# Input projection with one 512-column matmul for the high weights and seven banks drained by ScalarE

## The chip, the core and the metric

The kernel runs on one core of a Trainium2 chip. Its engines work side by side: PE (TensorE) multiplies, DVE (VectorE), ACT (ScalarE) and POOL (GpSimd) work element by element, SP (SyncE) issues the transfers. The metric is the device time of one execution in microseconds (us), as the median of the runs.

## The reference

The model has two layers on a sequence of 512 tokens with 2048 features, in float32. Only the first line of the first layer is touched by the change: a projection from 2048 to 8192 features, whose first half (`u`) is pooled over the sequence and whose second half gates it.

```
h = rmsnorm(x, norm_g)
proj = h @ w_in                       # (512, 2048) @ (2048, 8192)
u, gate = proj[..., :W_A], proj[..., W_A:]
pooled = causal_mean_pool(u, w) - u   # windows 2, 4, 8, 16 by group
y = einsum(pooled, w_group) * scale * silu(gate)
x = x + y @ w_out
# then the second layer: keys and values, latent attention, output projection
```

## The kernel before

**Numbers in two parts.** A float32 operand is split into a high part in PE's reduced float32 format (`hi`, written by ACT as a cast) and the rest (`lo`, written by DVE as a subtraction). A product is then three matmuls: high by high, high by low, low by high.

**Seven products instead of eight.** The projection multiplies blocks of 2x2 in the manner of Strassen and Winograd. The 64 output tiles (128 features by 512 tokens) are taken in pairs. Two of the 32 pairs are computed plainly in an opening stage, which also loads x and builds its seven combinations for each of the 8 blocks j of the inner dimension (`xh[j]`, `xl[j]`: 128 partitions, seven pieces of 256 tokens). The other 30 pairs follow in a loop (`n` = 0 to 29, pairs 18 to 31 and then 0 to 15). A pair has four quarters (`q`), each of two blocks j.

For each quarter `w_combos` loads 2 x 256 KB of weights into `raw` (three buffers), adds up four combinations (two in one instruction on DVE, line 301, then two on POOL, lines 303 and 304), casts all seven to `hi` on ACT (line 307) and subtracts to `lo` on DVE (line 308); `hi` and `lo` have two buffers each. `seven` then issues 42 matmuls of 256 columns (lines 324, 326, 328): seven products, two blocks, three matmuls each. The products gather in four banks of PSUM (`k0` to `k3`; two products to a bank, seven halves used), each with two buffers.

When the last quarter of a pair is done, `gather` adds the seven sums up: ACT copies one (line 334), DVE adds the others to it straight from PSUM (lines 335 to 338) into the tile `e` (two buffers), and SP stores two output tiles to DRAM (line 347). For the last loads, pairs 0 to 3 (`n` = 14 to 17), DVE also pools the outputs before they are stored (`pool_tile`, lines 240 to 256). The first eight rounds also square x on ACT and add the squares on DVE; in round 8 DVE works out the norm from them (lines 155 to 160 and 168).

**Order.** Each engine runs its own queue in order. The order of each queue is laid down when the program is built, by a scheduler that goes through a modelled timeline; waits are by semaphores between the engines. A tile's buffer is reused when all that used it has finished.

Of the kernel before, what the change touches and what calls it, by code (L numbers as in the profile page):

```python
# [51 lines left out]
def trunk_kernel(  # L52
# [50 lines left out]
    def dram():  # L103
        return dpool.tile([P, S], F32, tag="scr", name="scr", bufs=64)
# [154 lines left out]
    with ExitStack() as c1:  # L259
        xcp = c1.enter_context(tc.tile_pool(name="xcp", bufs=NJ))  # L260
        w7 = c1.enter_context(tc.tile_pool(name="w7", bufs=2, **tile_))
        ps7 = c1.enter_context(tc.tile_pool(name="ps7", bufs=2, space=bass.MemoryType.PSUM))
        xh, xl = [None] * NJ, [None] * NJ

        def x_load(j):

# [4 lines left out]

        def x_parts(j, c, hp):

            h = xcp.tile([P, 7, H], F32R, tag="xh", name="xh")
            lo = xcp.tile([P, 7, H], F32R, tag="xl", name="xl")
            xh[j], xl[j] = h, lo
            h12 = hp.tile([P, H], F32R, tag="h12", name="h12", bufs=NJ)
            l12 = hp.tile([P, H], F32R, tag="l12", name="l12", bufs=NJ)
            A.activation(c[:, 2:8:5, :], c[:, 2:8:5, :], AF.Copy, scale=cs[:, C_GA + 2 * j:C_GA + 2 * j + 1])
            A.activation(c[:, 0:2, :], c[:, 0:2, :], AF.Copy, scale=cs[:, C_GA + 2 * j + 1:C_GA + 2 * j + 2])  # L280
            A.copy(h[:, 0:3, :], c[:, 0:3, :])
            V.tensor_tensor(lo[:, 0:3, :], c[:, 0:3, :], f(h[:, 0:3, :]), ALU.subtract)
            split(c[:, 7, :], h12, l12)
            return h12, l12

        def x_sums(j, c):
            h, lo = xh[j], xl[j]
            V.tensor_tensor(c[:, 3:5, :], c[:, 1:3, :], c[:, 7:8, :].broadcast_to([P, 2, H]), ALU.subtract)
            V.scalar_tensor_tensor(c[:, 5, :], c[:, 4, :], -1.0, c[:, 1, :], ALU.mult, ALU.subtract)
            V.scalar_tensor_tensor(c[:, 6, :], c[:, 5, :], -1.0, c[:, 0, :], ALU.mult, ALU.subtract)  # L290
            A.copy(h[:, 3:7, :], c[:, 3:7, :])
            V.tensor_tensor(lo[:, 3:7, :], c[:, 3:7, :], f(h[:, 3:7, :]), ALU.subtract)

        def w_combos(pair, q):

            c = w7.tile([P, 2, 8, P], F32, tag="raw", name="raw", bufs=3)
            for m in range(2):
                nc.sync.dma_start(c[:, :, 2 - 2 * m:4 - 2 * m, :],
                                  awin[2 * pair + m][:, q * S:(q + 1) * S].rearrange(
                                      "p (j k n) -> p j k n", j=2, k=2))  # L300
            V.tensor_tensor(c[:, :, 4:6, :], c[:, :, 0:1, :].broadcast_to([P, 2, 2, P]),  # L301
                            c[:, :, 1:3, :], ALU.add)
            G.tensor_tensor(c[:, :, 6, :], c[:, :, 4, :], c[:, :, 2, :], ALU.add)  # L303
            G.tensor_tensor(c[:, :, 7, :], c[:, :, 6, :], c[:, :, 3, :], ALU.add)
            hi = w7.tile([P, 2, 7, P], F32R, tag="hi", name="hi")
            lo = w7.tile([P, 2, 7, P], F32R, tag="lo", name="lo")
            A.copy(hi, c[:, :, 1:8, :])  # L307
            V.tensor_tensor(lo, c[:, :, 1:8, :], f(hi), ALU.subtract)  # L308
            return hi, lo

        def banks():
            return [ps7.tile([P, 2, H], F32, tag=f"k{i}", name=f"k{i}") for i in range(4)]


        SEVEN = ((2, 0, 0, 0), (0, 6, 1, 0), (1, 2, 2, 0), (3, 4, 3, 0),
                 (5, 5, 0, 1), (6, 1, 1, 1), (4, 3, 2, 1))

        def seven(ks, w, j):
            hi, lo = w
            for wi, xi, b, h in SEVEN:  # L320
                dst = ks[b][:, h, :]
                first, last = j == 0 and h == 0, j == NJ - 1

                T.matmul(dst, hi[:, j % 2, wi, :], xh[j][:, xi, :], start=first, stop=False,  # L324
                         skip_group_check=True)
                T.matmul(dst, hi[:, j % 2, wi, :], xl[j][:, xi, :], start=False, stop=False,  # L326
                         skip_group_check=True)
                T.matmul(dst, lo[:, j % 2, wi, :], xh[j][:, xi, :], start=False, stop=last,  # L328
                         skip_group_check=True)

        def gather(ks, pair):

            e = epool.tile([P, 7, H], F32, tag="e", name="e")
            A.copy(e[:, 6, :], ks[2][:, 0, :])
            V.tensor_tensor(e[:, 0:2, :], e[:, 6:7, :].broadcast_to([P, 2, H]), ks[0], ALU.add)
            V.tensor_tensor(e[:, 2, :], e[:, 1, :], ks[2][:, 1, :], ALU.add)
            V.tensor_tensor(e[:, 3:6:2, :], e[:, 1:3, :], ks[3][:, 0:1, :].broadcast_to([P, 2, H]), ALU.add)
            V.tensor_tensor(e[:, 4:7:2, :], e[:, 2:4, :], ks[1], ALU.add)
            for i, v in enumerate((e[:, 0:7:6, :], e[:, 4:6, :])):
                o = 2 * pair + i  # L340
                raws[o] = dram()
                if i:
                    neg.add(o)
                if o < 8:
                    nc.sync.dma_start(raws[o], pool_tile(v, i == 1, WINS[0]))
                else:
                    nc.sync.dma_start(raws[o].rearrange("p (h t) -> p h t", h=2), v)


        accs = [ps7.tile([P, 2, H], F32, tag=f"k{i}", name=f"k{i}") for i in range(4)]  # L350
        with ExitStack() as c2:
            hp = c2.enter_context(tc.tile_pool(name="hp", bufs=2, **tile_))
            for j in range(NJ):
                c = x_load(j)
                raw = hp.tile([P, 4, 2, P], F32, tag="hraw", name="hraw")
                hi = w7.tile([P, 4, 2, P], F32R, tag="hi", name="hi")
                lo = w7.tile([P, 4, 2, P], F32R, tag="lo", name="lo")
                for o in range(4):
                    nc.sync.dma_start(raw[:, o, :, :], awin[32 + o][:, 2 * j * P:2 * (j + 1) * P].rearrange(
                        "p (k n) -> p k n", k=2))  # L360
                h12, l12 = x_parts(j, c, hp)
                for o in (0, 2):
                    split(raw[:, o:o + 2], hi[:, o:o + 2], lo[:, o:o + 2])
                x_sums(j, c)
                a, b = xh[j], xl[j]
                for o in range(4):
                    for dst, k, h, l in ((accs[o][:, 0, :], 0, a[:, 2, :], b[:, 2, :]),
                                         (accs[o][:, 1, :], 0, h12, l12),
                                         (accs[o], 1, a[:, 0:2, :], b[:, 0:2, :])):
                        first = j == 0 and h is not h12 and k == 0  # L370
                        T.matmul(dst, hi[:, o, k, :], h, start=first, stop=False, skip_group_check=True)
                        T.matmul(dst, hi[:, o, k, :], l, start=False, stop=False, skip_group_check=True)
                        T.matmul(dst, lo[:, o, k, :], h, start=False, stop=j == NJ - 1 and k == 1,
                                 skip_group_check=True)
        epool = c1.enter_context(tc.tile_pool(name="epool", bufs=2, **tile_))
        tp[0] = c1.enter_context(tc.tile_pool(name="tpool1", bufs=6, **tile_))
        for o in range(0, 4, 2):
            e = epool.tile([P, 7, H], F32, tag="e", name="e")
            for i in range(2):
                v = e[:, 2 * i:2 * i + 2, :]  # L380
                A.copy(v, accs[o + i])
                raws[32 + o + i] = dram()
                nc.sync.dma_start(raws[32 + o + i].rearrange("p (h t) -> p h t", h=2), v)

        sq = [tt_(), tt_()]

# [7 lines left out]
                V.tensor_tensor(sq[k % 2], sq[k % 2], x, ALU.add)  # L394

        for n, pair in enumerate((*range(18, 32), *range(16))):
            ks = banks()
            for q in range(NJ // 2):
                w = w_combos(pair, q)
                seven(ks, w, 2 * q)  # L400
                seven(ks, w, 2 * q + 1)
            if n < 8:
                square(2 * n)
                square(2 * n + 1)
            if n == 8:
                V.tensor_tensor(sq[0], sq[0], sq[1], ALU.add)
                p = ps7.tile([P, 2, H], F32, tag="k3", name="k3").rearrange("p h t -> p (h t)")
                ra[0] = norm_r(sq[0], D, p)
            gather(ks, pair)
# [526 lines left out]
```

## Time and profile before

| | |
|---|---|
| median of three runs | 1963.8 us (1961.78 to 1964.49) |
| the profiled execution | 1961.67 us, of which the span is 1959.9 us |
| granted PE clock | 0.999 |
| PE busy | 1933.3 us (99%), 11324 matmuls |
| DVE busy | 1280.2 us (65%) |
| ACT busy | 815.1 us (42%) |
| POOL busy | 262.9 us (13%) |

Rows of the page and of the groups read: line, engine, operation, output and inputs, shape, count, then busy us and mean ns. Rows of a timeline read: start in us from the span's start, duration in us, engine, line, operation, output and inputs; in square brackets stands how long the engine idled before and what ended that. Rows by stage read: the window, its length, then busy us and instruction counts of PE, PE's weight loads, DVE, ACT and POOL, then the granted clock and the transfers. The projection's loop runs from 55.5 to 667 us of the span.

### The profile page before, as it was taken

Reading aid. Unit: us, or ns where it says so; the run is one execution under the profiler, and the core shown is the slowest. Engines: PE = TensorE matmul, PEld = TensorE weight load, DVE = VectorE, ACT = ScalarE, POOL = GpSimd, SP = SyncE. Lnnn points to the kernel's source line nnn. Section 1 sums busy time; section 2 is a strip of 40 time slices with the busy share of each in tenths; the row PEclk is TensorE's granted clock in tenths of the full one; section 3 lists DMA queues with packets and bytes.
Section 4 is the critical chain, followed back from the end, with each engine's and each line's share of the span. In section 5 each row is a group of like instructions: output and inputs, shape, how many; then the busy total and the mean of one; then the engine's idle time right before and its main releaser. Section 6 shows DMA issues by size and latency. Waiting matters only on the chain.

```text
span 1959.9 us, 30545 instructions
## 1 busy us (share of the span) xinstructions
PE 1933.3 (99%) x11324; PEld 1707.0 (87%) x11324; DVE 1280.2 (65%) x2305; ACT 815.1 (42%) x1553; POOL 262.9 (13%) x404
## 2 busy tenths in 40 slices
PE   8999999999999999999999999999999999999999
PEld 7899999999999888888888888888888888878887
DVE  8766676797666587485694567573345888786432
ACT  7533333333333443333323454332245677774221
POOL 0432332334332100000000000000010111210000
PEclk9999999999999999999999999999999999999999
DMA  6644344435444464344344343233332111111632
GB/s 198 201 135 138 119 140 130 129 120 173 140 128 132 162 205 148 113 124 140 118 126 139 113 145 123 87 97 97 97 92 75 46 38 59 52 58 46 217 119 86
DMA packets 168134, 235.51 MB, mean 120 GB/s; under 512 B 14897, under 2 KB 95153, under 8 KB 167985
## 3 DMA queue, kind: packets, MB, share of 16 engines
q1 hardware_dynamic: 167696, 233.37, 37.9%
q8 instruction: 88, 1.44, 0.3%
q14 instruction: 62, 0.50, 0.1%
q10 hardware_dynamic: 288, 0.20, 0.0%
HBM read 208.35 MB, written 25.17 MB: 119 GB/s over the span
## 4 chain that ended last, share of the span: by engine, by line
PE 93%; DVE 3%; DMA 2%; issue 1%; ACT 1%; SPq 0%; DVEq 0%; ACTq 0%
PE mm L142 16%; PE mm L140 16%; PE mm L141 16%; PE k L328 9%; PE k L324 9%; PE k L326 9%; PE sc L728 3%; PE mm L604 1%; PE mm L602 1%; PE mm L603 1%; PE tr L687 1%; PE mm L622 1%; PE mm L624 1%; PE mm L623 1%; DVE lo L308 1%
## 5 line engine op out<-in xcount | busy, mean ns | idle before, releaser
L122 ACT CAST whi<-raw 128x512 fp32r<-128x512 f32 (+2 forms) x421 | 255.7, 611 | 518.9 <-PE mm L141 455.7
L324 PE MATMUL k<-xh,hi 128*128 128x256 f32 x1680 | 460.1, 283 | 0.1
L326 PE MATMUL k<-xl,hi 128*128 128x256 f32 x1680 | 460.0, 283 | 0.0
L123 DVE TENSOR_TENSOR wlo<-raw,whi 128x512 fp32r<-128x512 f32 (+2 forms) x421 | 281.9, 672 | 222.2 <-ACT whi L122 217.8
L328 PE MATMUL k<-xh,lo 128*128 128x256 f32 x1680 | 418.1, 284 | 3.9 <-DVE lo L308 3.9
L307 ACT CAST hi<-raw 128x1792 fp32r<-128x1792 f32 x120 | 202.8, 1690 | 373.5 <-PE k L328 258.2
L308 DVE TENSOR_TENSOR lo<-raw,hi 128x1792 fp32r<-128x1792 f32 x120 | 248.9, 2074 | 158.5 <-ACT hi L307 158.5
L142 PE MATMUL mm<-bt,wlo 128*128 128x512 f32 x860 | 335.3, 390 | 0.0
L140 PE MATMUL mm<-bt,whi 128*128 128x512 f32 x860 | 334.6, 389 | 0.0
L141 PE MATMUL mm<-bt,whi 128*128 128x512 f32 x860 | 334.4, 389 | 0.0
L324 PEld LDWEIGHTS k<-xh,hi 128*128 128x128 f32 x1680 | 322.5, 192 | 0.3 <-ACT hi L307 0.3
L326 PEld LDWEIGHTS k<-xl,hi 128*128 128x128 f32 x1680 | 322.5, 192 | 0.0
L328 PEld LDWEIGHTS k<-xh,lo 128*128 128x128 f32 x1680 | 296.7, 192 | 5.6 <-DVE lo L308 5.1
L140 PE MATMUL mm<-at,whi 128*128 128x512 f32 x516 | 201.7, 392 | 3.1 <-ACT whi L122 3.1
L142 PE MATMUL mm<-at,wlo 128*128 128x512 f32 x516 | 202.0, 392 | 2.2 <-DVE wlo L123 2.2
L141 PE MATMUL mm<-at,whi 128*128 128x512 f32 x516 | 201.8, 391 | 0.0
L142 PEld LDWEIGHTS mm<-bt,wlo 128*128 128x128 f32 x860 | 161.4, 188 | 34.3 <-issue 0.5
L140 PEld LDWEIGHTS mm<-bt,whi 128*128 128x128 f32 x860 | 161.4, 188 | 33.8 <-ACT whi L122 0.2
L141 PEld LDWEIGHTS mm<-bt,whi 128*128 128x128 f32 x860 | 161.4, 188 | 33.3
L303 POOL TENSOR_TENSOR raw<-raw 128x256 f32<-128x256 f32 x120 | 101.3, 844 | 437.3 <-DVE raw L301 414.7
L142 PEld LDWEIGHTS mm<-at,wlo 128*128 128x128 f32 x516 | 97.2, 188 | 24.1 <-DVE wlo L123 3.8
L140 PEld LDWEIGHTS mm<-at,whi 128*128 128x128 f32 x516 | 97.2, 189 | 23.6 <-ACT whi L122 3.7
(1152 smaller groups left out, 2573.4 us busy)
## 6 DMA issues: line engine op xcount, KB each, us to landing
raw<-awin SPq DMA_DIRECT2D x240, 256.0 KB, 3.2
raw<-awo SPq DMA_DIRECT2D x128, 256.0 KB, 2.8
raw<-bwin SPq DMA_DIRECT2D x80, 256.0 KB, 2.7
raw<-awg SPq DMA_DIRECT2D x64, 256.0 KB, 2.8
raw<-bwo SPq DMA_DIRECT2D x59, 256.0 KB, 2.8
scr<-e SPq DMA_DIRECT2D x56, 256.0 KB, 2.6
raw<-wkvb SPq DMA_DIRECT2D x32, 256.0 KB, 3.0
raw<-wqb SPq DMA_DIRECT2D x32, 192.0 KB, 2.4
```

The costliest lines, as they stand in the source:

```text
L122: A.copy(hi[:, :n], raw[:, :n])
L123: V.tensor_tensor(lo[:, :n], raw[:, :n], f(hi[:, :n]), ALU.subtract)
L140: T.matmul(dst, wh, xh, start=first, stop=False)
L141: T.matmul(dst, wh, xl, start=False, stop=False)
L142: T.matmul(dst, wl, xh, start=False, stop=last)
L303: G.tensor_tensor(c[:, :, 6, :], c[:, :, 4, :], c[:, :, 2, :], ALU.add)
L307: A.copy(hi, c[:, :, 1:8, :])
L308: V.tensor_tensor(lo, c[:, :, 1:8, :], f(hi), ALU.subtract)
L324: T.matmul(dst, hi[:, j % 2, wi, :], xh[j][:, xi, :], start=first, stop=False, skip_group_check=True)
L326: T.matmul(dst, hi[:, j % 2, wi, :], xl[j][:, xi, :], start=False, stop=False, skip_group_check=True)
L328: T.matmul(dst, lo[:, j % 2, wi, :], xh[j][:, xi, :], start=False, stop=last, skip_group_check=True)
L728: T.matmul(s[:, 0:n], l, r, start=(j == 0), stop=(j == 4))
```

## The change

The high and the low part of x now lie side by side in one tile (`xc[j]`: seven pieces of 2 x 256), so one matmul of 512 columns multiplies the high weights by both. Its two halves go to the two halves of a bank, and the third matmul (low weights by high x, 256 columns) is added to the second half. Each product therefore needs a bank of its own: seven banks per pair, out of eight in rotation under one name `k`. In the last quarter ACT copies each bank as it is finished into `e`, which is twice as wide (14 x 256) and has one buffer instead of two. DVE first adds the two halves of all seven in one instruction of 1792 elements, then adds up the outputs as before, all from `e`. The weight sums stay as they were, and so do the opening stage (but for the layout of x) and all that follows the projection.

```
-        ps7 = c1.enter_context(tc.tile_pool(name="ps7", bufs=2, space=bass.MemoryType.PSUM))
-        xh, xl = [None] * NJ, [None] * NJ
+        ps7 = c1.enter_context(tc.tile_pool(name="ps7", bufs=8, space=bass.MemoryType.PSUM))
+        xc = [None] * NJ
...
-            h = xcp.tile([P, 7, H], F32R, tag="xh", name="xh")
-            lo = xcp.tile([P, 7, H], F32R, tag="xl", name="xl")
+            xc[j] = xcp.tile([P, 7, 2, H], F32R, tag="xc", name="xc")
+            h, lo = xc[j][:, :, 0, :], xc[j][:, :, 1, :]
...
-        def seven(ks, w, j):
+        def seven(ks, w, q, e):
             hi, lo = w
-            for wi, xi, b, h in SEVEN:
-                dst = ks[b][:, h, :]
-                first, last = j == 0 and h == 0, j == NJ - 1
-                T.matmul(dst, hi[:, j % 2, wi, :], xh[j][:, xi, :], start=first, stop=False,
-                         skip_group_check=True)
-                T.matmul(dst, hi[:, j % 2, wi, :], xl[j][:, xi, :], start=False, stop=False,
-                         skip_group_check=True)
-                T.matmul(dst, lo[:, j % 2, wi, :], xh[j][:, xi, :], start=False, stop=last,
-                         skip_group_check=True)
+            for n, (wi, xi) in enumerate(SEVEN):
+                for i in range(2):
+                    x = xc[2 * q + i]
+                    T.matmul(ks[n], hi[:, i, wi, :], x[:, xi, :, :], start=q == 0 and i == 0, stop=False,
+                             skip_group_check=True)
+                    T.matmul(ks[n][:, 1, :], lo[:, i, wi, :], x[:, xi, 0, :], start=False,
+                             stop=q == NJ // 2 - 1 and i == 1, skip_group_check=True)
+                if q == NJ // 2 - 1:
+                    m = 2 * PLACE[n]
+                    A.copy(e[:, m:m + 2, :], ks[n])
...
-            e = epool.tile([P, 7, H], F32, tag="e", name="e")
-            A.copy(e[:, 6, :], ks[2][:, 0, :])
-            V.tensor_tensor(e[:, 0:2, :], e[:, 6:7, :].broadcast_to([P, 2, H]), ks[0], ALU.add)
-            V.tensor_tensor(e[:, 2, :], e[:, 1, :], ks[2][:, 1, :], ALU.add)
-            V.tensor_tensor(e[:, 3:6:2, :], e[:, 1:3, :], ks[3][:, 0:1, :].broadcast_to([P, 2, H]), ALU.add)
-            V.tensor_tensor(e[:, 4:7:2, :], e[:, 2:4, :], ks[1], ALU.add)
+            V.tensor_tensor(e[:, 0:14:2, :], e[:, 0:14:2, :], e[:, 1:14:2, :], ALU.add)
+            V.tensor_tensor(e[:, 2:5:2, :], e[:, 0:1, :].broadcast_to([P, 2, H]), e[:, 2:5:2, :], ALU.add)
+            V.tensor_tensor(e[:, 6, :], e[:, 4, :], e[:, 6, :], ALU.add)
+            V.tensor_tensor(e[:, 0:14:13, :], e[:, 4:7:2, :], e[:, 12:13, :].broadcast_to([P, 2, H]), ALU.add)
+            V.tensor_tensor(e[:, 8:11:2, :], e[:, 0:7:6, :], e[:, 8:11:2, :], ALU.add)
...
-        epool = c1.enter_context(tc.tile_pool(name="epool", bufs=2, **tile_))
+        epool = c1.enter_context(tc.tile_pool(name="epool", bufs=1, **tile_))
```

In the lists of order, `x7x256` is the 7-fold add, line 301 before and line 300 after is DVE's weight sum, and a number behind a name tells one tile from the next of the same kind. On DVE, the gather of round 11 before the change stands in one block between the split of one quarter and the next:

```order
L308 TENSOR_TENSOR lo_3438<-raw_3431,hi_3437 128x1792
L301 TENSOR_TENSOR raw_3535<-raw_3535 128x2x256
L335 TENSOR_TENSOR e_3365<-e_3365,k0_3153 128x512
L336 TENSOR_TENSOR e_3365<-e_3365,k2_3155 128x256
L337 TENSOR_TENSOR e_3365<-e_3365,k3_3156 128x2x256
L338 TENSOR_TENSOR e_3365<-e_3365,k1_3154 128x2x256
L308 TENSOR_TENSOR lo_3490<-raw_3483,hi_3489 128x1792
```

After the change, DVE's gather of round 11 (`e_2821`) is spread over the next round, whose second, third and fourth splits are `lo_3043`, `lo_3081` and `lo_3119`:

```order
L307 TENSOR_TENSOR lo_3043<-raw_3036,hi_3042 128x1792
L335 TENSOR_TENSOR e_2821<-e_2821 128x7x256
L307 TENSOR_TENSOR lo_3081<-raw_3074,hi_3080 128x1792
L337 TENSOR_TENSOR e_2821<-e_2821 128x2x256
L300 TENSOR_TENSOR raw_3174<-raw_3174 128x2x256
L338 TENSOR_TENSOR e_2821<-e_2821 128x256
L307 TENSOR_TENSOR lo_3119<-raw_3112,hi_3118 128x1792
L339 TENSOR_TENSOR e_2821<-e_2821 128x2x256
L300 TENSOR_TENSOR raw_3212<-raw_3212 128x2x256
L340 TENSOR_TENSOR e_2821<-e_2821 128x2x256
L307 TENSOR_TENSOR lo_3181<-raw_3174,hi_3180 128x1792
```

The last add, on which the stores of `e` wait, has moved behind three splits. On ACT, the drain of that round stood before the change as one copy between two casts:

```order
L307 CAST hi_3437<-raw_3431 128x1792
L334 COPY e_3365<-k2_3155 128x256
L307 CAST hi_3489<-raw_3483 128x1792
L307 CAST hi_3541<-raw_3535 128x1792
L307 CAST hi_3607<-raw_3601 128x1792
```

After the change ACT has six copies, the cast for the next round's second quarter (`hi_3042`), and the seventh copy:

```order
L306 CAST hi_3004<-raw_2998 128x1792
L331 COPY e_2821<-k_2814 128x512
L331 COPY e_2821<-k_2815 128x512
L331 COPY e_2821<-k_2816 128x512
L331 COPY e_2821<-k_2817 128x512
L331 COPY e_2821<-k_2818 128x512
L331 COPY e_2821<-k_2819 128x512
L306 CAST hi_3042<-raw_3036 128x1792
L331 COPY e_2821<-k_2820 128x512
L306 CAST hi_3080<-raw_3074 128x1792
```

In the rounds 1, 8, 15 and 17 that cast stands ahead of all seven copies instead. On DVE, the stretch of round 16 between its second and third split (`lo_3603`, `lo_3641`) holds the gather of round 15 (`e_3365`) and part of its predecessor's pooling (lines 247 to 256):

```order
L307 TENSOR_TENSOR lo_3603<-raw_3596,hi_3602 128x1792
L300 TENSOR_TENSOR raw_3672<-raw_3672 128x2x256
L247 TENSOR_TENSOR tt__3352<-tt__3349 128x512
L253 SCALAR_TENSOR_TENSOR tt__3352<-tt__3352,cs_66 128x1
L256 SCALAR_TENSOR_TENSOR tt__3355<-tt__3352,tt__3349 128x512
L335 TENSOR_TENSOR e_3365<-e_3365 128x7x256
L300 TENSOR_TENSOR raw_3750<-raw_3750 128x2x256
L337 TENSOR_TENSOR e_3365<-e_3365 128x2x256
L338 TENSOR_TENSOR e_3365<-e_3365 128x256
L339 TENSOR_TENSOR e_3365<-e_3365 128x2x256
L340 TENSOR_TENSOR e_3365<-e_3365 128x2x256
L307 TENSOR_TENSOR lo_3641<-raw_3634,hi_3640 128x1792
```

Before the change, no two splits there had more than five instructions between them, and there was no 7-fold add.

More of the change, by code (lines that the diff above doesn't have):

```diff
@@ L347, in gather @@
                     nc.sync.dma_start(raws[o].rearrange("p (h t) -> p h t", h=2), v)
[L350 removed]
+        accs = [bank() for i in range(4)]
         with ExitStack() as c2:
@@ L396, in trunk_kernel @@
         for n, pair in enumerate((*range(18, 32), *range(16))):
-            ks = banks()
+            ks = [bank() for _ in range(7)]
+            e = epool.tile([P, 14, H], F32, tag="e", name="e")
             for q in range(NJ // 2):
-                w = w_combos(pair, q)
-                seven(ks, w, 2 * q)
-                seven(ks, w, 2 * q + 1)
+                seven(ks, w_combos(pair, q), q, e)
             if n < 8:
```

34 lines of the change are left out of this document (16 added, 18 removed).

## The prediction

> **What bounds the kernel now.** I read the busy table first, then the groups by line, then busy time by stage, then the timelines of single engines.
>
> ```profile
> PE 1933.3 (99%) x11324; PEld 1707.0 (87%) x11324; DVE 1280.2 (65%) x2305; ACT 815.1 (42%) x1553; POOL 262.9 (13%) x404
> ...
> L324 PE MATMUL k<-xh,hi 128*128 128x256 f32 x1680 | 460.1, 283 | 0.1
> ...
> PE k L328 <- DVE lo L308: 3.9, 6, 1.6
> ```
>
> PE is never free: in the projection its only wait for a weight is 3.9 us. A matmul's 283 ns is its own length; matmuls overlap, so the price of one is the spacing. Busy time by stage gives it: the first row is the projection (256 columns), the second the later projections (512 columns).
>
> ```profile
> 200.00:400.00 200.00, 199.77 (x1660) 199.09 (x1659) 145.20 (x145) 68.69 (x50) 63.91 (x83) 1.00 0.41 127
> ...
> 1000.00:1200.00 200.00, 200.00 (x884) 165.60 (x883) 127.94 (x200) 86.39 (x142) 0.33 (x3) 1.00 0.42 132
> ...
> 23.14 0.28 PE L373 MATMUL k<-h,lo 128*128 128x256 f32 x1
> 23.26 0.40 PE L371 MATMUL k<-xh,hi 128*128 128x512 f32 x1
> 23.49 0.40 PE L372 MATMUL k<-xl,hi 128*128 128x512 f32 x1
> 23.73 0.51 PE L373 MATMUL k<-xh,lo 128*128 128x512 f32 x2
> ...
> 55.53 0.28 PE L324 MATMUL k<-xh,hi 128*128 128x256 f32 x1
> ...
> 666.81 0.28 PE L328 MATMUL k<-xh,lo 128*128 128x256 f32 x1
> ```
>
> 200 us over 1660 and over 884 matmuls are 0.120 and 0.226 us. The opening stage, which mixes both widths, has 0.12 from the 256 to the next and 0.23 and 0.24 after a 512, in rows of two digits. The last two rows are the first and the last matmul of the loop. DVE is the second busiest here: 145 of 200 us. One quarter of a pair (q) on ACT, DVE, POOL and SP, with the drain of a pair inside it:
>
> ```profile
> 304.17 1.69 ACT L307 CAST hi<-raw 128x1792 fp32r<-128x1792 f32 x1 [3.35 <-PE k L328]
> ...
> 309.21 1.70 ACT L307 CAST hi<-raw 128x1792 fp32r<-128x1792 f32 x1 [3.08 <-issue]
> ...
> 305.89 2.02 DVE L308 TENSOR_TENSOR lo<-raw,hi 128x1792 fp32r<-128x1792 f32 x1 [2.41 <-ACT hi L307]
> 307.83 0.68 DVE L301 TENSOR_TENSOR raw<-raw 128x512 f32<-128x512 f32 x1
> 308.44 0.68 DVE L335 TENSOR_TENSOR e<-e,k 128x512 f32<-128x512 f32 x1
> 309.15 0.42 DVE L336 TENSOR_TENSOR e<-e,k 128x256 f32<-128x256 f32 x1
> ...
> 310.32 0.69 DVE L338 TENSOR_TENSOR e<-e,k 128x512 f32<-128x512 f32 x1
> ...
> 308.65 0.74 POOL L303 TENSOR_TENSOR raw<-raw 128x256 f32<-128x256 f32 x1 [3.48 <-DVE raw L301]
> ...
> 311.08 1.17 SPq L347 DMA_DIRECT2D scr<-e  x2
> ...
> scr<-e SPq DMA_DIRECT2D x56, 256.0 KB, 2.6
> ```
>
> The split of the weights (hi) repeats every 5.04 us = 42 x 0.120: PE sets the pace. hi waits until PE is done with the quarter two back (two buffers); lo starts 0.03 us after hi and DVE takes the next instruction 1.94 us later, 0.61 after one of 512 elements, some 0.35 after one of 256. Both stores issue in 1.17 us, 0.07 after the last add, and land 2.6 us after issue. Note that the drain add of 308.44 (one operand in PSUM) and the POOL sum of 308.65 overlap, and both keep their usual length.
>
> **The change, part by part.** *PE.* 1680 times, two matmuls of 256 become one of 512: 2 x 0.120 - 0.226 = 0.014 us, times 1680 = 23.5 us less, all on the path. A pair takes 56 x (0.226 + 0.120) = 19.4 us of PE instead of 168 x 0.120 = 20.2. The Trainium skill (TensorE: Matmul & The Clock Gate, Back-to-back issue gap) puts an isolated matmul at its columns over 2.4 GHz plus 2.5 ns; by that the gain would be 2.5 ns x 1680, an estimate of 4 us. The two spacings above give 0.414 ns per column and 14 ns per matmul beside them, so the trace speaks for the larger gain.
>
> *ACT.* Seven drains of 512 elements instead of one of 256.
>
> ```profile
> 55.03 0.59 ACT L381 COPY e<-k 128x512 f32<-128x512 f32 x1 [1.51 <-PE k L373]
> 55.53 1.69 ACT L307 CAST hi<-raw 128x1792 fp32r<-128x1792 f32 x1
> ```
>
> Such a copy blocks ACT for 0.50 us: 3.5 us more per pair beside 4 x 1.69. ACT is busy 69 of 200 us, so its sum costs nothing; its place in a chain does (below).
>
> *DVE.* Per pair, one add of 1792 elements more (1.94 us, as lo). 30 x 1.94 = 58 us more on an engine with 55 free in 200, so not a bound by its sum. But all of the gather now has both operands in SBUF. What that means stands in these rows, DVE and POOL side by side:
>
> ```profile
> 379.27 0.68 DVE L256 SCALAR_TENSOR_TENSOR tt__4044<-tt__4041,tt__4038 128x512 f32<-128x512 f32 x1
> 379.88 1.23 DVE L240 SCALAR_TENSOR_TENSOR tt__4048<-e,r 128x512 f32<-128x512 f32 x1
> ...
> 379.49 1.07 POOL L303 TENSOR_TENSOR raw<-raw 128x256 f32<-128x256 f32 x1 [3.05 <-DVE raw L301]
> ...
> 260.54 2.56 DVE L308 TENSOR_TENSOR lo<-raw,hi 128x1792 fp32r<-128x1792 f32 x1 [1.00 <-ACT hi L307]
> ...
> 260.49 0.74 POOL L304 TENSOR_TENSOR raw<-raw 128x256 f32<-128x256 f32 x1
> ```
>
> A DVE instruction from SBUF alone that comes while POOL works waits: 1.23 for 0.69, 2.56 for 2.02, each 0.54 us. POOL, coming second, waits for DVE (1.07 for 0.74). They exclude each other; the older gather with its PSUM operand was exempt. So each POOL sum (8 per pair) costs DVE up to 0.54 us when DVE is busy. The Trainium skill (SBUF — State Buffer, Who interferes with whom) states the same exclusion and the same exemption; by it, too, the sum goes against this change.
>
> *The ring through e.* The order has one e buffer where there were two, so the first drain of a pair waits until the last pair's stores have landed, and in the order the gather is spread between the lo instructions of the next round (rounds 2 to 14). One lap, from the first drain to the next pair's: six drains 3.0; hi 1.72 (ACT has it behind them); lo, 7-fold add, lo 3 x 1.94 = 5.82; add 0.61, weight sum 0.61, add 0.35; lo behind the first POOL sum that follows 1.94 + 0.54; add behind the second 0.61 + 0.54; weight sum 0.61; last add 0.76; second store 0.58; landing 2.6. Sum 20.3 us against PE's 19.4. Without the two POOL waits it would be 19.2 and hidden. The first laps of each run eat the lead; I count nine that cost, 9 x 0.9 = 8 us. From round 18 on the order has the last adds before the third lo: the lap is shorter by more than 2.5 us there and costs nothing.
>
> *Four places with more on DVE.* Where DVE also does other work, count its queue from one round's third lo to the next round's. The plain round: 4 lo 7.8, 7-fold add 1.9, 4 weight sums 2.4, small adds 2.2, POOL waits 8 x 0.54 = 4.3: 18.6, under 19.4. Four stretches also hold a second gather's small adds (2.2; in round 9 half of them), a fifth weight sum (0.6) and its two POOL waits (1.1): 3.9 and 2.8. On top of that come, in rounds 16 and 18, eight pooling instructions
>
> ```profile
> 378.40 0.15 DVE L253 SCALAR_TENSOR_TENSOR tt__4041<-tt__4041,cs 128x1 f32<-128x1 f32 x1
> ...
> L158 DVE TENSOR_TENSOR tt__2685<-r 128x512 f32<-128x512 f32 x3 | 2.6, 865 | 0.0
> ```
>
> (6 x 0.61 + 2 x 0.15 = 4.0), in all 26.5; in round 9 the norm's ten of 512 elements and one of 0.4 (6.6), in all 28.0; in round 2 four adds of the squares (2.4), in all 24.9. Less 19.4 these are 7.1, 7.1, 8.6 and 5.5 us, 28; a few POOL sums will fall where DVE idles, and I take 26. There the first drain also stands behind the next pair's second hi on ACT, and PE waits for its bank; that is inside these sums. Rounds 17 and 19 inherit about 1 us each: 2. Before, the same extra work met a DVE that was 6 us per round freer (no 7-fold add, no POOL waits): the projection took 666.8 - 55.5 = 611.3 us for 5040 x 0.120 = 604.8, so all its stalls were 6.5, of which some 4.3 are the start, which stays, and 2.2 go.
>
> *The clock after a long wait, and the end.* PE's spacing behind a gap of 2.5 us:
>
> ```profile
> 669.62 0.50 PE L140 MATMUL mm<-at,whi 128*128 128x512 f32 x1 [2.54 <-ACT whi L122]
> ...
> 671.61 0.79 PE L142 MATMUL mm<-at,wlo 128*128 128x512 f32 x1 [1.25 <-DVE wlo L123]
> 672.20 0.63 PE L140 MATMUL mm<-at,whi 128*128 128x512 f32 x1
> 672.62 0.63 PE L141 MATMUL mm<-at,whi 128*128 128x512 f32 x1
> ...
> 675.12 0.39 PE L141 MATMUL mm<-at,whi 128*128 128x512 f32 x1
> ...
> 91.84 0.74 PE L328 MATMUL k<-xh,lo 128*128 128x256 f32 x4 [1.64 <-DVE lo L308]
> ```
>
> 0.42 instead of 0.226 until 675: about 1.3 us lost; the 1.64 us gap had no such tail (its four matmuls are 0.12 apart, 0.74 in all). The four places will have waits of both sizes: 0 to 6 us, I take 4. At the end of the projection seven drains and a 1.94 us add precede the next stage's first splits: 0 to 2, I take 1. The loads of weights and the later stages keep their instructions and their order.
>
> Sum: 1961.7 (the profiled execution; 1959.9 of it is the span) - 23.5 + 8 + 26 + 2 - 2.2 + 4 + 1 = 1977. The three runs' median lies 2.1 above that execution, so I forecast 1979.
>
> **Rivals.** *PE's gain arrives (faster).* If POOL's hold does not bite the new adds, laps are 19.2 and the four stretches 5.4 shorter, 19.5 to 22.6, costing 7: 1961.7 - 23.5 + 7 - 2.2 + 1 = 1944, or 1946 as a median. It decides where a POOL sum costs DVE less than about 0.25 us instead of 0.54: then the lap falls to 19.7 and the places to half. For it: POOL's sums have 4 us of slack and may fall where DVE idles. Against: every row of two SBUF operands that came during a POOL sum waited.
> *Half of it.* At 0.27 a sum the laps lose 3 and the four places 15: 1961.7 - 23.5 + 3 + 15 + 1 - 2.2 + 3 + 1 = 1959, as a median 1961: no change.
> *A longer lap.* Weights land later than stores did; if loads just ahead of the stores let these land as late, 0.6 us more, twelve laps cost 1.5 instead of nine 0.9: 10 more, 1989; where the loads slip too, DVE's weight sums wait in the same laps, another half microsecond each: 1995.
>
> ```profile
> raw<-awin SPq DMA_DIRECT2D x240, 256.0 KB, 3.2
> ```
>
> *The wide matmul saves nothing.* At the 0.24 us of the opening stage's last row a 512 costs two of 256: 1979 + 23.5 = 2002. The average over 884 speaks against it. By the rule named above it would be 1979 + 19 = 1998.
>
> **How the numbers follow.** Forecast with its own range 1968 to 1988: 0.54. Gain arrives: 0.13. Half: 0.08. Longer lap: 0.20. No saving per matmul: 0.05. Faster is 0.13, no change 0.08 (within 0.2%, 4 us, about what a measurement of this kernel can tell), slower 0.79. The range 1962 to 1996 leaves out most of the first rival and the last.
>
> **What would show it.** Right: 512-column rows 0.226 apart and 256 ones 0.12; a projection of about 623 us; DVE's lo and e adds at 2.5 and 1.2 us where POOL runs; the first drain of a pair waiting for the store of e; PE waits of 2 to 5 us for lo or for a bank near rounds 2, 9, 16 and 18, and rounds of 19.4 us after the twentieth. Wrong: e adds that keep 0.68 and 2.02 us, or rounds of 19.4 us throughout, or spacings over 0.13 for the 256.

## Result and the profile after

The changed kernel is slower: 2008.8 us as the median of four runs (2006.3 to 2011.2) against 1962.8 (1961.0 to 1964.5) for the kernel before, ratio 1.0232 with a 95% interval of 1.022 to 1.0245. The forecast, 1979 (1962 to 1996), had the sign and part of the mechanism, and was 30 us short.

The page's busy line and the groups of the changed kernel that answer to those shown of before (line, engine, operation, shape, count, then busy us and mean ns, then idle time just before and what ended it; line 325 is the wide matmul, 327 the narrow one, 307 lo, 331 the drain):

```profile
PE 1945.6 (97%) x9644; PEld 1624.9 (81%) x9644; DVE 1387.0 (69%) x2335; ACT 911.4 (45%) x1733; POOL 385.6 (19%) x404
...
L325 PE MATMUL k<-xc,hi 128*128 128x512 f32 x1680 | 563.2, 402 | 20.9 <-ACT e L331 17.9 <-ACT hi L306 3.0
...
L327 PE MATMUL k<-xc,lo 128*128 128x256 f32 x1680 | 388.6, 287 | 21.5 <-DVE lo L307 21.1
...
L307 DVE TENSOR_TENSOR lo<-raw,hi 128x1792 fp32r<-128x1792 f32 x120 | 267.3, 2229 | 19.1 <-ACT hi L306 19.0
```

PE, whose only wait for a weight in the loop was 3.9 us before, now waits for drains and for lo. All of the loss lies in the projection's loop. Its first and last matmul after the change:

```profile
55.49 1.08 PE L325 MATMUL k<-xc,hi 128*128 128x512 f32 x4
...
716.61 0.28 PE L327 MATMUL k<-xc,lo 128*128 128x256 f32 x1
```

The loop, from the start of its first matmul to that of its last, takes 661.1 us against 666.81 - 55.53 = 611.3 before. What follows it takes 2009.4 - 716.6 = 1292.8 us against 1293.1. By stage (busy us and counts of PE, weight loads, DVE, ACT, POOL, then the granted clock, the DMA share and GB/s):

```profile
55.00:155.00 100.00, 87.59 (x455) 72.62 (x453) 73.99 (x62) 48.54 (x58) 49.40 (x34) 0.93 0.51 155
155.00:255.00 100.00, 96.58 (x530) 82.01 (x531) 78.36 (x62) 48.90 (x54) 45.63 (x38) 0.98 0.40 120
255.00:355.00 100.00, 89.72 (x491) 76.29 (x490) 82.42 (x69) 45.31 (x51) 49.81 (x36) 0.98 0.41 122
355.00:455.00 100.00, 94.64 (x504) 79.62 (x504) 84.58 (x74) 46.71 (x49) 44.09 (x38) 0.95 0.36 111
455.00:555.00 100.00, 93.54 (x507) 78.48 (x506) 85.22 (x76) 46.97 (x52) 49.19 (x40) 0.97 0.47 141
555.00:655.00 100.00, 97.37 (x549) 82.98 (x548) 81.91 (x64) 48.63 (x54) 55.24 (x40) 1.00 0.43 128
```

At 0.346 us a pair of matmuls a full stretch would hold 578. The early ones hold 455 to 530, where the forecast expected most of the trouble; but the last one holds 549, which is a round of 112 matmuls in 20.4 us where it expected 19.4. DVE has 15 to 26 of 100 us free in each. That it idles while PE waits for it says: look at what it waits for, not at its work. The sums of waits (in all, times, longest) of the changed kernel that bear on this:

```profile
DVE raw L300 <- DMA raw<-awin: 106.8, 47, 4.8
...
ACT e L331 <- DMA scr<-e: 64.7, 23, 5.8
...
PE k L327 <- DVE lo L307: 21.1, 29, 3.3
...
PE k L325 <- ACT e L331: 17.9, 13, 2.9
```

and DVE's wait for loads in the kernel before:

```profile
DVE raw L301 <- DMA raw<-awin: 18.6, 12, 4.7
```

So there are two waits for transfers: ACT's drains wait for the stores of `e`, as forecast, and DVE's weight sums wait for loads of weights, which was not.

**An early round.** ACT, DVE and SP in the changed kernel, from the first drain of one pair to that of the next:

```profile
197.53 3.04 ACT L331 COPY e<-k 128x512 f32<-128x512 f32 x6 [3.40 <-DMA scr<-e]
200.40 1.75 ACT L306 CAST hi<-raw 128x1792 fp32r<-128x1792 f32 x1
...
218.36 3.03 ACT L331 COPY e<-k 128x512 f32<-128x512 f32 x6 [3.40 <-DMA scr<-e]
```

```profile
202.17 2.02 DVE L307 TENSOR_TENSOR lo<-raw,hi 128x1792 fp32r<-128x1792 f32 x1 [0.74 <-ACT hi L306]
204.12 2.56 DVE L335 TENSOR_TENSOR e<-e 128x1792 f32<-128x1792 f32 x1
206.60 2.01 DVE L307 TENSOR_TENSOR lo<-raw,hi 128x1792 fp32r<-128x1792 f32 x1
208.53 0.68 DVE L337 TENSOR_TENSOR e<-e 128x512 f32<-128x512 f32 x1
209.13 0.68 DVE L300 TENSOR_TENSOR raw<-raw 128x512 f32<-128x512 f32 x1
209.74 0.41 DVE L338 TENSOR_TENSOR e<-e 128x256 f32<-128x256 f32 x1
210.07 2.55 DVE L307 TENSOR_TENSOR lo<-raw,hi 128x1792 fp32r<-128x1792 f32 x1
212.55 1.22 DVE L339 TENSOR_TENSOR e<-e 128x512 f32<-128x512 f32 x1
213.70 0.68 DVE L300 TENSOR_TENSOR raw<-raw 128x512 f32<-128x512 f32 x1
214.30 0.68 DVE L340 TENSOR_TENSOR e<-e 128x512 f32<-128x512 f32 x1
```

```profile
215.00 1.18 SPq L349 DMA_DIRECT2D scr<-e  x2
```

This is the ring through `e` in the order that the forecast listed, and it is closed: no engine in it is free between its steps. It takes 218.36 - 197.53 = 20.83 us. The forecast's 20.3 lacks the hold of the 7-fold add (2.48 us from 204.12 to 206.60, not 1.94).

**A late round.** DVE, ACT and SP of the changed kernel after the twentieth round:

```profile
588.57 2.01 DVE L307 TENSOR_TENSOR lo<-raw,hi 128x1792 fp32r<-128x1792 f32 x1
590.50 0.68 DVE L300 TENSOR_TENSOR raw<-raw 128x512 f32<-128x512 f32 x1
591.11 2.01 DVE L307 TENSOR_TENSOR lo<-raw,hi 128x1792 fp32r<-128x1792 f32 x1
595.03 0.69 DVE L300 TENSOR_TENSOR raw<-raw 128x512 f32<-128x512 f32 x1 [1.91 <-DMA raw<-awin]
597.73 0.69 DVE L300 TENSOR_TENSOR raw<-raw 128x512 f32<-128x512 f32 x1 [2.01 <-DMA raw<-awin]
598.34 2.02 DVE L307 TENSOR_TENSOR lo<-raw,hi 128x1792 fp32r<-128x1792 f32 x1
```

```profile
594.91 1.75 ACT L306 CAST hi<-raw 128x1792 fp32r<-128x1792 f32 x1
```

```profile
588.67 1.18 SPq L349 DMA_DIRECT2D scr<-e  x2
590.61 10.66 SPq L297 DMA_DIRECT2D raw<-awin  x6
```

The lo that ends at 590.58 frees a `raw` buffer, the loads for it issue from 590.61, and its weight sum, which waits for them, starts at 595.03, 4.4 us later. That sum stands in DVE's queue ahead of the lo of 598.34, and so does the sum of the load after it. DVE idles 1.91 and 2.01 us with that lo behind it; its hi was ready at 596.66 (594.91 + 1.75), so it starts 1.7 us late. This is a second ring, through `raw`, and it too is longer than PE's 19.4 us: the rounds of this stretch take 20.4.

### The profile page after: what moved, and what is told of

Same layout as the page of the kernel before. It is cut to its first block, busy times and chain, and to the rows that moved or that the text cites. A ratio compares the mean times of both kernels' runs of the same rounds, so it can differ in the third digit from the quotient of the medians.

```text
span 2009.4 us, 27421 instructions
## 1 busy us (share of the span) xinstructions
PE 1945.6 (97%) x9644; PEld 1624.9 (81%) x9644; DVE 1387.0 (69%) x2335; ACT 911.4 (45%) x1733; POOL 385.6 (19%) x404
## 4 chain that ended last, share of the span: by engine, by line
PE 74%; DVE 12%; issue 5%; DMA 5%; ACT 3%; SPq 1%; DVEq 0%; ACTq 0%
PE mm L142 16%; PE mm L140 16%; PE mm L141 16%; PE k L325 7%; DVE lo L307 5%; PE k L327 4%; PE sc L728 3%; DMA raw<-awin 3%; DVE e L335 2%; DMA scr<-e 2%; PE mm L604 1%; PE mm L602 1%; PE mm L603 1%; ACT e L331 1%; PE tr L687 1%
## 5 line engine op out<-in xcount | busy, mean ns | idle before, releaser
L325 PE MATMUL k<-xc,hi 128*128 128x512 f32 x1680 | 563.2, 402 | 20.9 <-ACT e L331 17.9
L327 PE MATMUL k<-xc,lo 128*128 128x256 f32 x1680 | 388.6, 287 | 21.5 <-DVE lo L307 21.1
L327 PEld LDWEIGHTS k<-xc,lo 128*128 128x128 f32 x1680 | 323.4, 192 | 70.8 <-DVE lo L307 40.9
L325 PEld LDWEIGHTS k<-xc,hi 128*128 128x128 f32 x1680 | 314.8, 192 | 67.9 <-ACT e L331 22.6
L307 DVE TENSOR_TENSOR lo<-raw,hi 128x1792 fp32r<-128x1792 f32 x120 | 267.3, 2229 | 19.1 <-ACT hi L306 19.0
L302 POOL TENSOR_TENSOR raw<-raw 128x256 f32<-128x256 f32 x120 | 155.3, 1294 | 368.4 <-DVE raw L300 314.9
L303 POOL TENSOR_TENSOR raw<-raw 128x256 f32<-128x256 f32 x120 | 172.9, 1441 | 9.2
L300 DVE TENSOR_TENSOR raw<-raw 128x512 f32<-128x512 f32 x120 | 86.7, 723 | 106.8 <-DMA raw<-awin 106.8
L331 ACT COPY e<-k 128x512 f32<-128x512 f32 x210 | 109.5, 615 | 76.6 <-DMA scr<-e 64.7
```

Of the source, the lines that this page charges most:

```text
L325: T.matmul(ks[n], hi[:, i, wi, :], x[:, xi, :, :], start=q == 0 and i == 0, stop=False, skip_group_check=True)
L327: T.matmul(ks[n][:, 1, :], lo[:, i, wi, :], x[:, xi, 0, :], start=False, stop=q == NJ // 2 - 1 and i == 1, skip_group_check=True)
L331: A.copy(e[:, m:m + 2, :], ks[n])
```

## Experiments

Theories A to E are those of the expectations: A, DVE's queue paces the rounds; A1 and A2, POOL's hold or the amount of work is what counts on DVE; B, drains and `e` pace everything; C, the wide matmul is not cheaper; D, the ring through `e` binds the early rounds; E, the ring through `raw` holds DVE at its sums. All are edits of the changed kernel except the control, whose base is the kernel before. The loop's length is taken from PE's rows as above, what follows it is the span less that point.

| kernel | median us | ratio to before, 95% | loop us | after the loop us |
|---|---|---|---|---|
| before | 1962.8 | | 611.3 | 1293.1 |
| changed | 2008.8 | 1.0232 (1.022 to 1.0245) | 661.1 | 1292.8 |
| without the 7-fold add | 1960.8 | 0.9988 (0.9979 to 0.9997) | 610.4 | 1292.5 |
| all sums on DVE | 2031.9 | 1.0345 (1.0328 to 1.0362) | 682.1 | 1293.0 |
| own output tile | 2003.2 | 1.0201 (1.0186 to 1.0217) | 645.6 | 1301.8 |
| fourth raw buffer | 2015.4 | 1.0261 (1.0246 to 1.0276) | 654.5 | 1303.4 |
| sums in own tile | 2001.5 | 1.0197 (1.0182 to 1.0212) | 641.8 | 1294.2 |
| both own tiles | 1970.8 | 1.0040 (1.0026 to 1.0054) | 604.9 | 1302.1 |
| sums in own tile, all on DVE | 1981.7 | 1.0100 (1.0084 to 1.0115) | 624.3 | 1293.1 |
| both own tiles, all sums on DVE | 1962.4 | 1.0001 (0.9992 to 1.0011) | 596.0 | 1303.1 |
| the same, new start | 1954.6 | 0.9959 (0.9946 to 0.9971) | 595.1 | 1301.8 |
| the same, without the gather's adds | 1938.7 | 0.9879 (0.9864 to 0.9894) | 587.5 | 1293.4 |
| before with the new sums | 1955.3 | 0.9965 (0.9952 to 0.9979) | 605.5 | 1293.1 |
| new start and new end | 1946.7 | 0.9917 (0.9903 to 0.993) | 594.8 | 1294.0 |

**Without the 7-fold add.**

```
-            V.tensor_tensor(e[:, 0:14:2, :], e[:, 0:14:2, :], e[:, 1:14:2, :], ALU.add)
```

> The changed kernel without the 7-fold add (1792 elements, 30 times), which joins the two halves of each product; everything else stays, so its output is not the sum wanted. Theory A (DVE's queue paces the rounds, by work and by what it waits for): each round loses 2.5 us of DVE time, all rounds fall to PE's 19.4 us, the half-rate clock behind long waits goes with the waits, and the time is near 1945 (1937 to 1960). Rival B (the seven drains on ACT and the single e buffer pace the rounds, whatever DVE does): PE keeps waiting for drains, 1990 to 2009. Rival C (a wide matmul costs as much as two narrow ones): not under 1962.

1960.8: B falls. C is passed by 1.2 us only; what speaks against it is the last stretch (555 to 655), which holds 571 matmuls, 0.35 us a pair. But the time is 0.8 us outside A's range and 16 over its middle, the loop is 29 us over PE's own 581.3 (1680 x 0.346), and DVE still waits 107.1 us for loads: work on DVE was not all.

**All weight sums on DVE.**

```
-            G.tensor_tensor(c[:, :, 6, :], c[:, :, 4, :], c[:, :, 2, :], ALU.add)
-            G.tensor_tensor(c[:, :, 7, :], c[:, :, 6, :], c[:, :, 3, :], ALU.add)
+            V.tensor_tensor(c[:, :, 6, :], c[:, :, 4, :], c[:, :, 2, :], ALU.add)
+            V.tensor_tensor(c[:, :, 7, :], c[:, :, 6, :], c[:, :, 3, :], ALU.add)
```

> The changed kernel with the two weight sums of POOL given to DVE: POOL is idle in the loop, DVE has eight instructions of 256 elements (0.35 us each) more per round. Theory A1 (what slows DVE is the wait for POOL's hold of SBUF, up to 0.54 us a sum, eight sums a round): 4.3 us of waits go and 2.8 us of work come, and a sum of POOL's 1.3 to 1.4 us becomes one of 0.4 on the way to the cast; laps shorten by about 1 to 1.5 us where they bind, 1975 to 1995. Rival A2 (DVE simply has too much work, POOL's hold costs little): 2.8 us more in each round that binds, 2030 to 2080. Rival B (drains and e): within 5 us of 2009.

2031.9, the number of A2, but not for its reason: DVE is busy 78 of 100 us in the stretch from 555 to 655, less than in the changed kernel, and PE completes 488 matmuls there. DVE waits for loads 121.8 us, 78 times. More of its queue now hangs on a load.

**The outputs in a tile of their own.**

```
+            t = opool.tile([P, 5, H], F32, tag="o", name="o")
-            V.tensor_tensor(e[:, 2:5:2, :], e[:, 0:1, :].broadcast_to([P, 2, H]), e[:, 2:5:2, :], ALU.add)
+            V.tensor_tensor(t[:, 0:2, :], e[:, 0:1, :].broadcast_to([P, 2, H]), e[:, 2:5:2, :], ALU.add)
...
-            for i, v in enumerate((e[:, 2:9:6, :], e[:, 10:14:3, :])):
+            for i, v in enumerate((t[:, 0:3:2, :], t[:, 1:5:3, :])):
```

> The changed kernel with the small adds written to a tile of their own (5 x 256), from which the stores go: the tile e is free after the last add and not 3.2 us later when its stores have landed. Theory D (the ring through e with its stores binds only in rounds 3 to 14, where a lap is 21 us): those laps fall by at least 0.6 us to what the load ring allows (20.3), the later rounds stay at 20.4; 1993 to 2002. Rival B (the ring through e paces all rounds): 20 rounds lose 1 us or more each, 1970 to 1990. Rival (e's stores don't matter): 2006 to 2011.

2003.2, just over the range of D: the loop is 15.5 us shorter, but 9 us are lost behind it (below). The waits for the stores of `e` are gone, those of DVE for loads stay (105.9 us), and the last stretch still holds 553 matmuls. The gain is not where D looked for it, though: the rounds 3 to 14 without round 9 are 21.2 us over PE's pace together, against 21.6 in the changed kernel, and what became shorter are the rounds 2, 9, 16 and 18 (the table under "Both tiles").

**A fourth raw buffer.**

```
+            p, b = (w8, 1) if (4 * n + q) % 4 == 3 else (w7, 3)
-            c = w7.tile([P, 2, 8, P], F32, tag="raw", name="raw", bufs=3)
+            c = p.tile([P, 2, 8, P], F32, tag="raw", name="raw", bufs=b)
...
-        tp[0] = c1.enter_context(tc.tile_pool(name="tpool1", bufs=6, **tile_))
+        tp[0] = c1.enter_context(tc.tile_pool(name="tpool1", bufs=4, **tile_))
```

> The changed kernel with a fourth buffer for the raw weights (the tiles for pooling go from six buffers to four to make room), so that a load starts a quarter earlier. Theory E (the load of the third buffer's successor is late, and its weight sum, which stands ahead of the next lo in DVE's queue, holds DVE for 1.8 us twice a round): the waits of DVE for loads go from 107 us to under 40, rounds from the nineteenth on take 19.4 to 19.6 us instead of 20.4, and the early ones shorten too; 1985 to 1998. Rival (DVE's waits for loads are slack that another wait takes up): 2004 to 2012.

A miss: 2015.4, and DVE's waits for loads did not fall (111.7 us). The loop is 6.6 us shorter than in the changed kernel, but 10.6 us are lost behind it, where PE waits 15.0 us. DVE's rows in a late round:

```profile
585.86 2.01 DVE L308 TENSOR_TENSOR lo<-raw,hi 128x1792 fp32r<-128x1792 f32 x1
589.80 0.69 DVE L301 TENSOR_TENSOR raw<-raw 128x512 f32<-128x512 f32 x1 [1.93 <-DMA raw<-awin]
592.36 0.69 DVE L301 TENSOR_TENSOR raw<-raw 128x512 f32<-128x512 f32 x1 [1.87 <-DMA raw<-awin]
592.97 2.02 DVE L308 TENSOR_TENSOR lo<-raw,hi 128x1792 fp32r<-128x1792 f32 x1
```

Two sums stand ahead of the same lo again, each just behind its load, so the fourth buffer did not move the sums back in DVE's queue. The run does not refute E, and does not show it either.

**The sums in a tile of their own.** The same 24 KB a partition, divided otherwise: a sum's buffer now comes free with the lo of two quarters before, which ties its place in the queue, while a load may run four ahead.

```
-            c = w7.tile([P, 2, 8, P], F32, tag="raw", name="raw", bufs=3)
+            c = wr.tile([P, 2, 4, P], F32, tag="raw", name="raw", bufs=4)
+            s = wr.tile([P, 2, 4, P], F32, tag="sum", name="sum", bufs=2)
...
-            A.copy(hi, c[:, :, 1:8, :])
-            V.tensor_tensor(lo, c[:, :, 1:8, :], f(hi), ALU.subtract)
+            for a, b, v in ((0, 3, c[:, :, 1:4, :]), (3, 7, s)):
+                A.copy(hi[:, :, a:b, :], v)
+                V.tensor_tensor(lo[:, :, a:b, :], v, f(hi[:, :, a:b, :]), ALU.subtract)
```

> The changed kernel with the weight sums in a tile of their own (two buffers of 4 KB) and the loaded weights in another (four of 4 KB, the same room in all): a sum now stands in DVE's queue behind the lo of two quarters before, while its load may start as soon as the lo of four quarters before is done, some 10 us ahead. lo and hi become two instructions each (about 0.07 us more per quarter on DVE). The opening stage's raw x has the room until the loop starts, which may cost 0 to 3 us at its start. Theory E (DVE stands in its queue at sums whose loads are late; the fourth buffer of the run before did not help since the order used it to put each sum still closer behind its load): DVE's waits for loads fall from 107 us to under 25, rounds from the twentieth on take 19.4 to 19.7 us, the early ones fall to the lap through e, about 20.3; 1982 to 1995. Rival (these waits are slack, DVE is held elsewhere): 2003 to 2012.

2001.5, of which 6.9 us are the late start (first matmul of the loop at 62.41 instead of 55.49). DVE's waits for loads fell from 106.8 us to 2.1 and the loop is 19.3 us shorter: that ring bound. (The edit also makes hi and lo in two pieces each, so that the first piece does not wait for the sums; the runs do not part this from the ring.) The rounds are not those of the forecast, though: rounds 4 to 7 ran at 19.5 to 19.6 us with the ring through `e` still there, and the late ones did not come to 19.4. The last stretch holds 528 matmuls, because the ring through `e` took over there. Its waits:

```profile
ACT e L333 <- DMA scr<-e: 67.4, 17, 5.4
...
PE k L327 <- ACT e L333: 31.4, 17, 5.1
```

**Both tiles.**

> The weight sums in a tile of their own, and the outputs too: both rings are cut. Theory E and D together (the two rings make the rounds long, the rest is the four places with more DVE work): early rounds come to 19.4 to 19.8 us as well, and with fewer long waits the granted clock stays at 1.00; what is left is about 25 us at the four places over the 1936 that PE alone would take: 1955 to 1975. Rival (the rings hide DVE's waits for POOL, which now appear): 1980 to 1995.

1970.8, in the range of the forecast, but not made up as forecast: 6.9 us of it are the late start and 9.0 the time lost behind the loop, while the four places and the rounds that inherit cost 12 us where some 25 were expected. The last stretch holds 576 matmuls, which is PE's pace. Cut alone, the rings give 15.5 and 19.3 us of loop; cut together 661.1 - 604.9 = 56.2, more than their sum. PE's rows, counted in rounds of a pair (168 matmuls before, 112 after), say where. The table has the us over PE's own pace (20.2 a round before, 19.4 after); rounds 2, 9, 16 and 18 are the four places of the prediction, 17 and 19 those that inherit.

| kernel | rounds 0, 1 | 2, 9, 16, 18 | 17, 19 | other 22 | all |
|---|---|---|---|---|---|
| before | 5.2 | 0.5 | 0.1 | 0.7 | 6.5 |
| changed | 7.3 | 32.1 | 5.4 | 35.0 | 79.8 |
| own output tile | 9.3 | 12.3 | 7.0 | 35.6 | 64.3 |
| sums in own tile | 5.1 | 17.4 | 1.3 | 36.8 | 60.5 |
| both own tiles | 5.1 | 6.0 | 6.2 | 6.3 | 23.6 |
| both own tiles, all sums on DVE | 4.6 | 2.4 | 2.4 | 5.3 | 14.7 |

In the 22 other rounds either cut alone gains nothing and both together 29 us: each ring alone is enough to hold them. Which rounds a ring holds differs from kernel to kernel; the scheduler lays the queues anew for each.

**POOL's hold, with the load ring cut** (the two sums on DVE, as in the second experiment):

> The weight sums in a tile of their own, all four of them on DVE, POOL idle. It tells what POOL's hold costs when no load stands in the way. Theory A1 (the hold costs up to 4.3 us a round where DVE binds, more than the 2.8 us of work that POOL takes off): 3 to 20 us below the run with the sums in a tile of their own and two of them on POOL. Rival A2 (work counts, the hold falls mostly into idle time): 10 to 30 us above it.

> Both rings cut, and all four weight sums on DVE. Theory A1: 3 to 20 us below the run with both rings cut and two sums on POOL, the fastest of the four, 1945 to 1965. Rival A2: 10 to 30 us above it.

19.8 us below the run with the sums in a tile of their own, and 8.4 us below the run with both tiles: A1, twice. The larger half of lo with POOL at work (both tiles) and, second, without:

```profile
L309 DVE TENSOR_TENSOR lo<-sum,hi 128x1024 fp32r<-128x1024 f32 x120 | 187.0, 1558 | 3.1 <-ACT hi L308 3.1
```

```profile
L309 DVE TENSOR_TENSOR lo<-sum,hi 128x1024 fp32r<-128x1024 f32 x120 | 145.8, 1219 | 1.3 <-ACT hi L308 1.3
```

0.34 us an instruction go to the hold. The gain need not be the hold's alone: ACT waited 37.0 us for POOL's second sum in the run with the sums in a tile of their own, and a shorter way from the load to the cast may have its share; the runs do not part the two. The same edit that cost 23 us with the load ring closed gains here, so what that run priced was the ring and not the hold.

**A new start, the floor, and a control.** The first moves the pool of x's raw tiles below the opening stage's other tiles, so that the loop's first loads find free room. The second leaves out the gather's adds. The third puts the new sums, all on DVE, and the new start into the kernel before.

> The kernel with both rings cut and all sums on DVE, with the places in SBUF laid out anew so that the first weight loads of the loop don't wait for the tiles of the opening stage's last matmuls. In the run before it PE waited 6.7 us there and went on at a granted clock of 0.97 for the first 100 us. If that start is what kept it from gaining: 5 to 9 us less, 1953 to 1958, faster than the kernel before by 0.2 to 0.5%. If the start stall only moves into the next quarters: 1960 to 1964.

> The same kernel without the eight adds that make the outputs from the drained banks (what is stored are unjoined products), so DVE has 4.5 us less per round: it shows the floor that PE and the rest of the chain set. Theory A: all rounds at PE's own 19.4 us, 1936 to 1946. Rival C (a wide matmul costs more than 0.226 us in this kernel): 1955 or more.

> The kernel before, with narrow matmuls and its own gather, but with the weight sums in a tile of their own and all on DVE. A control: if PE alone bounds the kernel before, it stays within 5 us of 1962 (its stalls in the projection are 6.5 us in all, of which 4.3 are the start). If the new arrangement helps by itself, 1950 to 1956, and what the run with both rings cut gains is not the wide matmul's.

The start is mended (1954.6). The floor is 1938.7, a stretch from 500 to 600 holding 577 matmuls: the wide matmul is as cheap as its spacing said. The control is the sobering one: the kernel before gains as much from the new arrangement (1955.3; its loop comes to 605.5 us, where PE alone takes 604.8), so at this point the wide matmul had brought nothing that the runs can tell. The difference lies behind the loop: PE's first wait there,

```profile
663.84 1.22 PE L140 MATMUL mm<-at,whi 128*128 128x512 f32 x2 [13.51 <-ACT at L145]
```

13.5 us where the kernel before waits 2.5. The next stage's work tiles lay in SBUF across the end of `e`, so their loads came after the loop's last store.

**A new end.**

```
+    ctx.enter_context(tc.tile_pool(name="gap", bufs=1, **tile_)).tile([P, H], F32, tag="gap", name="gap")
     tp[0] = ctx.enter_context(tc.tile_pool(name="tpool2", bufs=6, **tile_))
```

> The run with the new start, and 1 KB left empty ahead of the next stage's work tiles in SBUF, so that they no longer share a place with the tile e. In that run the loop took 595.1 us against 611.3 before, but what follows it took 8.7 us longer: the next stage's first loads stood behind the last store of the loop, and PE waited 13.5 us instead of 2.5. If that is all: 8 to 10 us less than 1954.6, 1944 to 1948, faster than the kernel before by about 0.8%, and 8 to 10 us below the control with narrow matmuls and new sums, which is what the wide matmul then brings. If the loop's last round pays for it instead: 1950 to 1956.

```profile
653.94 0.49 PE L140 MATMUL mm<-at,whi 128*128 128x512 f32 x1 [2.75 <-ACT whi L122]
```

1946.7, 0.8% below the kernel before, and 8.7 us below the control. That is what the wide matmul nets here, of the 20 that PE gives. The rest is still in the loop, which is 13.5 us over PE's 581.3 here, and 6.2 over it without the gather's adds.

## Why the prediction failed, step by step

By the terms of its sum the forecast has a loop of 625.6 us; it took 661.1. By the table above, 27 of the 35.5 us between lie in the 22 rounds that are not places (35.0, where the sum had 8 for nine laps), 9.5 in the places and the rounds that inherit (37.5 for 28) and 3 in the first two rounds (7.3 for 4.3); 4 go off again, since the sum had the clock apart.

- *PE, -23.5.* Right, a little large. The rows of the changed kernel

```profile
559.80 0.40 PE L325 MATMUL k<-xc,hi 128*128 128x512 f32 x1
560.04 0.40 PE L327 MATMUL k<-xc,lo 128*128 128x256 f32 x2
560.27 0.40 PE L325 MATMUL k<-xc,hi 128*128 128x512 f32 x1
```

  have 0.47 us for one wide and two narrow matmuls, 0.226 + 2 x 0.12. From the full stretches (836 narrow matmuls in 100 us before, 577 in the floor run) it is (3 x 100/836 - 2 x 100/577) x 1680 = 20.5. The formula that the Trainium skill (TensorE: Matmul & The Clock Gate, Back-to-back issue gap) has for an isolated matmul, which gave 4, does not fit these streams.
- *DVE and POOL exclude each other.* Right: the 7-fold add, 2.01 us at its fastest, takes 2.56 in the round shown. The exclusion is the one that the Trainium skill states (SBUF — State Buffer, Who interferes with whom). With POOL idle the loop is 17.5 us shorter where the ring through `e` stands (641.8 to 624.3), 8.9 where it is cut (604.9 to 596.0).
- *The ring through e, +8: mis-sized.* The lap shown was built as forecast, 20.83 us instead of 20.3, since one hold was left out. But it did not act alone: cutting it alone gives 15.5 us, hardly any of it in the rounds that were to pay (35.6 us against 35.0 in the other 22), with the load ring cut 641.8 - 604.9 = 36.9.
- *The step that failed:* "The loads of weights and the later stages keep their instructions and their order", and from round 18 on the ring "costs nothing". The loads kept their instructions, but they follow the lo that frees their buffer, their sums stand in DVE's queue ahead of another lo, and the gather fills the room that DVE had to wait in. Before, DVE could wait 18.6 us for loads without PE noticing; now it is 106.8 and PE does. The late rounds are 20.4 us. The forecast counted what each instruction takes on DVE and let each queue move on when its own sum allowed; it never walked DVE's queue past a load. The third rival ("where the loads slip too, DVE's weight sums wait in the same laps") named the mechanism, at half a microsecond a lap and a chance of 0.20. The 22 rounds that had 8 us in the sum are 35.0 over PE's pace, and 6.3 with both rings cut.
- *Four places with more DVE work, +26, and 2 inherited.* The size was nearly right, 32.1 and 5.4 us, but in part by luck. It was worked out from DVE's instructions and POOL's hold alone, and with both rings cut and POOL still at work only 6.0 and 6.2 us of it are left (2.4 and 2.4 with POOL idle): two thirds of it went with the rings.
- *The clock, +4: mis-sized.* PE's rows in the changed kernel:

```profile
155.22 0.50 PE L325 MATMUL k<-xc,hi 128*128 128x512 f32 x1 [2.87 <-ACT e L331]
...
156.53 0.63 PE L325 MATMUL k<-xc,hi 128*128 128x512 f32 x1
...
157.17 0.63 PE L325 MATMUL k<-xc,hi 128*128 128x512 f32 x1
...
159.09 0.63 PE L325 MATMUL k<-xc,hi 128*128 128x512 f32 x1
...
159.69 0.39 PE L325 MATMUL k<-xc,hi 128*128 128x512 f32 x1
```

  A pair takes 0.64 us instead of 0.35 for some 3.4 us: about 1.6 us lost by one wait. Added up over PE's rows, eight such stretches cost 15 us; the granted clock of the six stretches above (0.07 + 0.02 + 0.02 + 0.05 + 0.03 short of 1) bounds it at 19. They lie inside the rounds of the table, not beside them. In the last run the clock is 1.00 in all of them.
- *The end, +1.* Nothing (1292.8 against 1293.1). *ACT* costs nothing by its sum, as said; it waits.

## What to carry to other kernels

When an engine that idled gets more work, list what its idle time covered before adding up busy times: in an in-order queue, a wait for a transfer that was free becomes a link in the ring of every tile whose release stands behind it. Draw each ring of buffers as a lap (who frees, who refills, what stands in the queue between) and compare every lap with the pace of the bound engine; where two rings hold the same rounds they must be cut together, since in those rounds either cut alone gains nothing. A rearranged kernel needs the same rearrangement in the old kernel as its control, and its seams looked at: places in SBUF cost 6.9 us at the loop's start and 8.7 at its end.

## What was not expected of the hardware

- The half-rate clock follows a wait neither at once nor always. After the 2.87 us wait above PE ran at full pace for 1.1 us (155.22 to 156.3), then at half for 3.4. After a wait of 2.11 us at 262.45 no half-rate stretch came; after one of 2.04 us at 467.84, with one of 1.07 us three us before it, PE was at half pace from its first matmul, for 5.7 us. The Trainium skill (TensorE: Matmul & The Clock Gate, What's actually happening) has the throttle after an idle window of about 3.4 us; here less was enough, but not each time.
- POOL pays for the exclusion too: the second of its sums takes 1.45 us on average in the loop against 0.87 before, and its busy time rose from 262.9 to 385.6 us with the same number of instructions.
